# Merged gate and up products in the first SwiGLU, h stored by k-tile, half of the bias comparisons on ScalarE

## The chip, the cores and the metric

One NeuronCore of a Trainium2 chip runs the whole program in one launch. The metric is the device time of that launch in microseconds, the median of several runs. Engines are named as in the profile: PE (TensorE), DVE (VectorE), ACT (ScalarE), POOL (GpSimd), SP (SyncE, which issues most transfers).

## The reference

A decoder trunk of two layers on 256 tokens of width 1024, float32. Each layer is SwiGLU, token mixer, SwiGLU, every one behind an RMS norm and an adaLN shift, scale and gate computed from `c`:

```
h = modulate(rms_norm(x, g), shift, scale)
x = x + 0.5 * gate * ((silu(h @ w_gate) * (h @ w_up)) @ w_down)      # d_ff 2816, four of them
```

The mixer of layer 0 is causal attention with 16 heads and a T5 bias (32 buckets of the distance between positions, a learned row of 16 head values for each bucket); that of layer 1 is multi-head latent attention with a shared K/V. The adaLN vectors are `silu(c) @ ada_w`, eighteen products of a vector with a 1024x1024 matrix besides two for the shared K/V.

## The kernel before

All large products keep float32 accuracy by splitting both operands into a high part and a low part (`F32R`, the type that PE takes for the fast float32 pass): `hi` is an ACT copy rounded to the type (line 628 for weights, 772 for activations), `lo` is the DVE difference (lines 629, 773). A product is then hi·hi + hi·lo + lo·hi. Weights stream once from HBM through `raw` (3 buffers, 1 MB each), are split, and are used.

**SwiGLU (`ffn`, line 886).** The hidden dimension is done in tiles f of 128 rows, 22 of them. For a tile, gate and up are each a sum over 8 k-tiles of 128. The weight tile is stationary and h, transposed (features on partitions, 256 tokens in the free dimension), streams through. There are two ways to do one k-tile:

- `mm3` (line 756) makes three matmuls of 256 columns, all into one half of a PSUM bank (gate in one half, up in the other).
- `mm2` (line 860) makes a *merged* pair: w_hi against h_hi and h_lo side by side (512 columns, line 863), then w_lo against h_hi (256 columns, line 864) into the second half. A product then fills a whole bank, gate and up need two, and `units` (line 894) has to add the two halves: an ACT copy and a DVE addition for each (lines 904, 905).

`MERGED` (line 30) says which SwiGLUs are merged: three of four; the first one, (0, 0), is not. PSUM has four banks for these products (`ps_mm`, line 534).

`h` is one tile `[P, 2, NT, D]` (line 844): hi then lo, each with two halves of 128 tokens, each half 1024 wide by k. So the 512 columns of one k-tile lie in four runs of 128 elements, the 256 columns of one part in two.

**The first SwiGLU** starts in `first` (line 1481): tiles f0 to f5 while the first weights, the adaLN rows of (0, 0) and h are being made. Tiles f6 to f21 follow in the loop of line 944. In the same stretch the **bias** of the attention is built (`bias_steps`, line 1117): 64 DVE comparisons (line 1179, one for each of 32 keys in two blocks) write rows of zeros and ones in bfloat16, 288 small bfloat16 matmuls (line 1164, three for each comparison and query block) multiply them by a table of differences, ACT copies the result out (line 1168), POOL masks the diagonal, and it goes to DRAM.

**adaLN rows** are 512 KB transfers (line 655) and one DVE pass each (line 639 or 677), handed out evenly over PE's estimated time by `ada_pace` (line 712): 40 of them over 172 us in the first SwiGLU.

**Order.** `Order` (line 243) sorts every engine's instructions at build time with estimated durations, so the order on each engine is fixed when the program runs; an instruction whose input is late holds up all behind it on its engine.

Of the kernel before, what the change touches and what calls it, by code (L numbers as in the profile page):

```python
# [21 lines left out]
P = 128  # L22
# [7 lines left out]
MERGED = ((0, 1), (1, 0), (1, 1))  # L30
# [97 lines left out]
def lay_out(v):  # L128
# [37 lines left out]
    out["tab"] = np.concatenate([np.tile(table[1:], (4, 1)), np.tile(table[:-1], (4, 1)), *keys], axis=1)  # L166
# [356 lines left out]
def trunk(ctx: ExitStack, tc: tile.TileContext, a: dict, out: bass.AP):  # L523
# [304 lines left out]
    def split_h(h, c0, n, z):  # L828
        cs = slice(c0, c0 + n)
        h[2].update(range(c0 // P, (c0 + n) // P))  # L830
        return split_evac(h[0][:, cs], h[1][:, cs], z)
# [10 lines left out]
    def new_h(t):  # L842
        if t == 0:
            both = hp.tile([P, 2, NT, D], F32R, tag="h", name=nm("h"))
            pair[:] = [both[:, 0], both[:, 1], both]
        return pair[0][:, t, :], pair[1][:, t, :], set(), list(pair)

    def hk(h, k):
        until(lambda: k in h[2])
        return kslice(h[0], k), kslice(h[1], k)  # L850
# [35 lines left out]
    def ffn(layer, idx, h, after, ada_to, start=None):  # L886

        last = (layer, idx) == (1, 1)
        with ExitStack() as st:
# [4 lines left out]
            def units(f, gate, up=None):  # L894


                g = gp.tile([P, NT, P], F32, tag="gT", name=nm("g"), bufs=2)
                if up is None:
                    gate, up = gate[:, 0], gate[:, 1]
                    nc.scalar.activation(g, gate, AF.Silu)  # L900
                else:
                    u = gp.tile([P, NT, P], F32, tag="uT", name=nm("u"), bufs=2)
                    for x, ps in ((g, gate), (u, up)):
                        nc.scalar.activation(x, ps[:, 1], AF.Copy)
                        nc.vector.tensor_tensor(x, ps[:, 0], x, op=ALU.add)
# [3 lines left out]
                gh, gl = [gq.tile([P, NT, P], F32R, tag=f"{nme}{f}", name=nm(nme)) for nme in ("gh", "gl")]  # L909
                split_evac(gh, gl, g)  # L910
                for t in range(NT):
                    gT[f, t] = gh[:, t, :], gl[:, t, :]
# [3 lines left out]
            ada_pace(ada_to, 90.0 if last else FFN_PACE)  # L916
# [27 lines left out]
            for f0 in range(B1 * P if start else FB, F, S):  # L944
# [8 lines left out]
                for f in range(f0 // P, (f0 + S) // P):  # L953
                    merged = (layer, idx) in MERGED
                    ps = [mm_tile().rearrange("p (i t q) -> p i t q", i=2, q=P) for _ in range(1 + merged)]
                    for i, pl in enumerate(parts):
                        for k in range(KD):
# [6 lines left out]
                            else:  # L964
                                mm3(ps[0][:, i], *w, *hs[:2], start=k == 0, stop=k == KD - 1)
# [31 lines left out]
    def attention(ap, g, qTs, kTs, vs, bias, oT, state, after_s=None):  # L997
# [64 lines left out]
        def av():  # L1062
# [11 lines left out]
            pov = po.rearrange("p r t q -> p t r q")  # L1074
            hi, lo = [x[:, :, kk * P:(kk + 2) * P].rearrange("p t (r q) -> p t r q", q=P) for x in oT[0][3][:2]]
            split_evac(hi, lo, pov)
# [36 lines left out]
    pieces = [cp.tile([P, 4, H], BF16, name=f"tab{i}") for i in range(3)]  # L1113
# [3 lines left out]
    def bias_steps():  # L1117

# [4 lines left out]
        with ExitStack() as st:  # L1123
# [3 lines left out]
            btab = bp.tile([P, 2 * H + NT * NB], F32, name="btab")  # L1127
            nc.sync.dma_start(btab, a["tab"])
            tab, prev = btab[:, :H], btab[:, H:2 * H]
            keyi = btab[:, 2 * H:].bitcast(I32).rearrange("p (t b) -> p t b", t=NT)  # L1130
# [13 lines left out]
            V.tensor_scalar(key, keyi, least, None, op0=ALU.add)  # L1144
            yield

            def parts():
# [56 lines left out]
    def moba(h, after):  # L1204
        with ExitStack() as st:
# [15 lines left out]
            oTp = [ap.tile([P, NT, D], F32R, name=f"oT{i}") for i in range(2)]  # L1221
            oT = [(oTp[0][:, t, :], oTp[1][:, t, :], set(), oTp) for t in range(NT)]
# [258 lines left out]
    def first(units):  # L1481
# [5 lines left out]
        with ExitStack() as st:  # L1487
            fp = st.enter_context(tc.tile_pool(name="fp", bufs=1))
            zeros = fp.tile([P, 512], BF16, name="zeros")
# [40 lines left out]
            for f in range(B1):  # L1530
                nc.tensor.matmul(accs[f], zeros[:, :P], zeros, start=True, stop=False)
            accs = [ps.rearrange("p (i t q) -> p i t q", i=2, q=P) for ps in accs]
# [14 lines left out]
            def transposed(k):  # L1547
                xT = ps_x[k % 2][:, :S]
                with ranked(2 * k + 1):
# [8 lines left out]
                    for i in range(fill if k == 1 else 0):  # L1558
                        nc.tensor.matmul(kslice(xT, 1), zeros[:, :P], zeros[:, :P], start=False, stop=i == fill - 1)
# [3 lines left out]
            for k in range(KD):  # L1563
                with ranked(2 * k + 2):
# [5 lines left out]
                    hh, hl = [x[:, :, k * P:(k + 1) * P] for x in h0[0][3][:2]]  # L1570
                    split_evac(hh, hl, z.rearrange("p (t q) -> p t q", q=P))
# [68 lines left out]
```

## Time and profile before

| | us |
|---|---|
| runs before, median of 3 | 1007.17 (1007.09 to 1007.45) |
| the profiled execution | 1007.52 |
| its span | 1005.7 |
| PE busy | 992.3 (99%), granted clock full throughout |
| DVE busy | 846.3 (84%) |
| ACT busy | 610.9 (61%) |
| POOL busy | 85.6 (9%) |
| HBM read | 255.34 MB, 258 GB/s over the span |

A matmul's duration in the trace runs from its issue to the modelled end of its pipeline, so durations of neighbours overlap; what a matmul takes from PE's time is the distance from its start to the start of the next. For DVE the same holds to a smaller degree.

### The profile page before, as it was taken

Reading aid. Unit: us, or ns where it says so; the run is one execution under the profiler, and the core shown is the slowest. Engines: PE = TensorE matmul, PEld = TensorE weight load, DVE = VectorE, ACT = ScalarE, POOL = GpSimd, SP = SyncE. Lnnn points to the kernel's source line nnn. Section 1 sums busy time; section 2 is a strip of 40 time slices with the busy share of each in tenths; the row PEclk is TensorE's granted clock in tenths of the full one; section 3 lists DMA queues with packets and bytes.
Section 4 is the critical chain, followed back from the end, with each engine's and each line's share of the span. In section 5 each row is a group of like instructions: output and inputs, shape, how many; then the busy total and the mean of one; then the engine's idle time right before and its main releaser. Section 6 shows DMA issues by size and latency. Waiting matters only on the chain.

```text
span 1005.7 us, 15693 instructions
## 1 busy us (share of the span) xinstructions
PE 992.3 (99%) x5814; PEld 852.2 (85%) x5814; DVE 846.3 (84%) x1435; ACT 610.9 (61%) x1105; POOL 85.6 (9%) x124
## 2 busy tenths in 40 slices
PE   8999999999999999999999999999999999999998
PEld 6999998888888788888888888888888878888886
DVE  8999998799889899999889999854998789767642
ACT  5663754378756875665358566643879786566521
POOL 3011100022231000000000000000144010000000
PEclk9999999999999999999999999999999999999999
DMA  9978899889785679897988998553343467544630
GB/s 353 403 279 290 324 359 351 311 303 334 267 318 200 253 277 326 327 333 270 374 311 312 336 326 339 191 211 108 105 147 131 168 228 276 208 168 168 225 131 21
DMA packets 54238, 260.55 MB, mean 259 GB/s; under 512 B 6289, under 2 KB 6801, under 8 KB 35986
## 3 DMA queue, kind: packets, MB, share of 16 engines
q1 hardware_dynamic: 52850, 256.06, 70.0%
q0 software_dynamic: 1024, 3.17, 1.0%
q8 instruction: 45, 0.74, 0.3%
q10 hardware_dynamic: 288, 0.33, 0.1%
q14 instruction: 31, 0.25, 0.1%
HBM read 255.34 MB, written 4.19 MB: 258 GB/s over the span
## 4 chain that ended last, share of the span: by engine, by line
PE 90%; DVE 5%; DMA 4%; ACT 1%; issue 0%; SPq 0%; POOL 0%; ACTq 0%; DVEq 0%
PE mm L863 20%; PE mm L757 17%; PE mm L759 17%; PE mm L758 17%; PE mm L864 10%; PE at L1014 2%; DMA adaw<-in_ada_dram 1%; DMA raw<-in_first_dram 1%; PE at L1070 1%; PE at L1050 1%; PE tr L1164 1%; DVE lo L629 1%; DMA raw<-in_w_dram 1%; PE tr L807 1%; PE tr L1438 0%
## 5 line engine op out<-in xcount | busy, mean ns | idle before, releaser
L629 DVE TENSOR_TENSOR lo<-raw,hi 128x1024 fp32r<-128x1024 f32 (+3 forms) x312 | 368.3, 1200 | 80.0 <-ACT hi L628 79.5
L628 ACT ACTIVATE hi<-raw 128x1024 fp32r<-128x1024 f32 (+3 forms) x312 | 318.5, 1039 | 163.0 <-PE mm L759 123.3
L863 PE MATMUL mm<-h,hi 128*128 128x512 f32 x864 | 302.4, 398 | 0.0
L864 PE MATMUL mm<-h,lo 128*128 128x256 f32 x864 | 237.1, 281 | 0.0
L863 PEld LDWEIGHTS mm<-h,hi 128*128 128x128 f32 x864 | 160.7, 188 | 37.8
L864 PEld LDWEIGHTS mm<-h,lo 128*128 128x128 f32 x864 | 162.2, 189 | 2.4
L639 DVE CUSTOM_DVE_ANT_0 adaw<-adaw,c_b,cols 128x1024 f32<-128x1024 f32 x112 | 141.6, 1281 | 0.7 <-DMA adaw<-in_ada_dram 0.7
L757 PE MATMUL mm<-hi,gh 128*128 128x512 f32 x352 | 137.5, 391 | 0.0
L758 PE MATMUL mm<-lo,gh 128*128 128x512 f32 x352 | 137.1, 389 | 0.0
L759 PE MATMUL mm<-hi,gl 128*128 128x512 f32 x352 | 137.1, 389 | 0.0
L757 PE MATMUL mm<-hi,h 128*128 128x512 f32 (+1 forms) x240 | 94.6, 399 | 0.8 <-ACT h L772 0.8
L759 PE MATMUL mm<-hi,h 128*128 128x512 f32 (+1 forms) x240 | 92.7, 392 | 1.6 <-DVE h L773 1.6
L758 PE MATMUL mm<-lo,h 128*128 128x512 f32 (+1 forms) x240 | 93.6, 393 | 0.0
L759 PEld LDWEIGHTS mm<-hi,gl 128*128 128x128 f32 x352 | 66.1, 188 | 13.8
L757 PEld LDWEIGHTS mm<-hi,gh 128*128 128x128 f32 x352 | 66.1, 188 | 13.5
L758 PEld LDWEIGHTS mm<-lo,gh 128*128 128x128 f32 x352 | 66.1, 188 | 13.4
L757 PE MATMUL mm<-h,hi 128*128 128x256 f32 x256 | 73.3, 290 | 0.1
L759 PE MATMUL mm<-h,lo 128*128 128x256 f32 x256 | 72.8, 287 | 0.2 <-DVE lo L629 0.2
L758 PE MATMUL mm<-h,hi 128*128 128x256 f32 x256 | 72.3, 286 | 0.0
L677 DVE SCALAR_TENSOR_TENSOR acc<-adaw,cols,acc 128x1024 f32<-128x1024 f32 x48 | 62.3, 1298 | 0.1
L759 PEld LDWEIGHTS mm<-hi,h 128*128 128x128 f32 x240 | 45.1, 188 | 10.6 <-DVE h L773 2.2
L757 PEld LDWEIGHTS mm<-hi,h 128*128 128x128 f32 x240 | 45.1, 188 | 9.6 <-ACT h L772 1.3
(233 smaller groups left out, 1463.4 us busy)
## 6 DMA issues: line engine op xcount, KB each, us to landing
raw<-in_w_dram SPq DMA_DIRECT2D x142, 1024.0 KB, 5.7
adaw<-in_ada_dram SPq DMA_DIRECT2D x160, 512.0 KB, 6.0
raw<-in_first_dram SPq DMA_DIRECT2D x24, 256.0 KB, 7.6
raw<-in_w_dram SPq DMA_DIRECT2D x12, 512.0 KB, 3.5
raw<-in_w_dram SPq DMA_DIRECT2D x6, 576.0 KB, 3.9
bias_d<-bt SPq DMA_DIRECT2D x12, 256.0 KB, 4.4
bg<-bias_d POOLq DMA_DIRECT2D x4, 768.0 KB, 6.3
raw<-in_w_dram SPq DMA_DIRECT2D x2, 768.0 KB, 4.3
```

What stands on the lines that cost most here:

```text
L628: nc.scalar.activation(hi, src, AF.Copy)
L629: nc.vector.tensor_tensor(lo, src, hi.bitcast(F32), op=ALU.subtract)
L639: nc.vector.tensor_tensor_reduce(wt, wt, c_b, 1.0, cols[:, i, c:c + 1], op0=ALU.mult, op1=ALU.add, accum_out=m_cols[:, i, c:c + 1])
L677: nc.vector.scalar_tensor_tensor(acc, ada_tile(j, k), cact[:, k:k + 1], acc, op0=ALU.mult, op1=ALU.add)
L757: nc.tensor.matmul(ps, lh, rh, start=start, stop=False)
L758: nc.tensor.matmul(ps, lh, rl, start=False, stop=False)
L759: nc.tensor.matmul(ps, ll, rh, start=False, stop=stop)
L807: nc.tensor.transpose(kslice(pt, j), kslice(y, j), ident)
L863: nc.tensor.matmul(ps, wh, h[2], start=start, stop=False)
L864: nc.tensor.matmul(ps[:, 1], wl, h[0], start=False, stop=stop)
L1014: nc.tensor.matmul(ps3[:, i, :], qTs(e, t), kTs(e, nk), start=bias is not None, stop=bias is not None or i == len(es) - 1)
L1050: nc.tensor.transpose(kslice(pt, i * (t + 1) + kb), ss[u][:, i, kb * P:(kb + 1) * P], ident)
```

## The change

- `MERGED` takes in the first SwiGLU, so its tiles f6 to f21 are done by `mm2` with two banks each.
- `h` becomes one tile `[P, KD, 2, NT, P]`: for each k-tile, hi and lo with both halves of the tokens lie in one run of 512 elements. The attention output `oT` of layer 0 gets the same layout. `units`, `first` and `hk_both` follow.
- Every second bias comparison (odd i) is an ACT `Sign` of query position minus key, giving -1 or 1; its table rows are halved and the constant that this leaves is taken out through another table column set, so there are two sets of `pieces`.
- `ada_pace` hands out no adaLN row in the first 40 us of PE time after `first`.
- `u` has one buffer in the first SwiGLU in place of two, `zeros` is 128 wide.

```diff
-MERGED = ((0, 1), (1, 0), (1, 1))
+MERGED = ((0, 0), (0, 1), (1, 0), (1, 1))
...
-    def ada_pace(vectors, us):
+    def ada_pace(vectors, us, wait=0.0):
         n = vectors * KD - ada_done[0]
-        pace[0] = us / n if n > 0 else None
-        pace[1] = clock[0] + (us / n if n > 0 else 0.0)
+        pace[0] = (us - wait) / n if n > 0 else None
+        pace[1] = clock[0] + wait + (pace[0] or 0.0)
...
-            both = hp.tile([P, 2, NT, D], F32R, tag="h", name=nm("h"))
-            pair[:] = [both[:, 0], both[:, 1], both]
-        return pair[0][:, t, :], pair[1][:, t, :], set(), list(pair)
+            pair[:] = [hp.tile([P, KD, 2, NT, P], F32R, tag="h", name=nm("h"))]
+        return pair[0][:, :, 0, t], pair[0][:, :, 1, t], set(), pair[0]
...
-        hh, hl, both = h[0][3]
-        ks = slice(k * P, (k + 1) * P)
-        return hh[:, :, ks], hl[:, :, ks], both[:, :, :, ks]
+        both = h[0][3][:, k].rearrange("p i t q -> p (i t q)")
+        return both[:, :S], both[:, S:], both
...
-        nc.tensor.matmul(ps[:, 1], wl, h[0], start=False, stop=stop)
+        nc.tensor.matmul(ps[:, S:], wl, h[0], start=False, stop=stop)
...
-                    u = gp.tile([P, NT, P], F32, tag="uT", name=nm("u"), bufs=2)
+                    u = gp.tile([P, S], F32, tag="uT", name=nm("u"), bufs=1 if start else 2)
...
-            ada_pace(ada_to, 90.0 if last else FFN_PACE)
+            ada_pace(ada_to, 90.0 if last else FFN_PACE, 40.0 if start else 0.0)
...
+            below = bp.tile([P, NT, NB], F32, name="below")
+            V.tensor_scalar(below, key, -1.0, 0.5, op0=ALU.mult, op1=ALU.add)
...
+                for signs in range(2):
+                    rows = bp.tile([P, 4, H], F32, tag="rows", name=nm("rows"))
+                    if signs:
+                        V.tensor_tensor(tab, tab, end, op=ALU.subtract)
+                    V.scalar_tensor_tensor(rows, blk[:, :, None].to_broadcast([P, 4, H]), 0.5 if signs else 1.0,
+                                           tab[:, None, :].to_broadcast([P, 4, H]), op0=ALU.mult, op1=ALU.mult)
+                    for i in range(3):
+                        V.tensor_copy(pieces[signs][i], rows)
+                        if i < 2:
+                            V.tensor_tensor(rows, rows, pieces[signs][i], op=ALU.subtract)
...
-                             oh[:, i, (t - kb) * P:(t - kb + 1) * P], pieces[pi], start=pi == 0, stop=pi == 2)
+                             oh[:, i, (t - kb) * P:(t - kb + 1) * P], pieces[i % 2][pi], start=pi == 0, stop=pi == 2)
...
-                        V.tensor_scalar(oh[:, i], posq[:, kb * P:], key[:, kb, 8 * c + i:8 * c + i + 1],
-                             None, op0=ALU.is_ge)
+                        m = 8 * c + i
+                        if i % 2:
+                            nc.scalar.activation(oh[:, i], posq[:, kb * P:], AF.Sign, bias=below[:, kb, m:m + 1])
+                        else:
+                            V.tensor_scalar(oh[:, i], posq[:, kb * P:], key[:, kb, m:m + 1], None, op0=ALU.is_ge)
```

The order on the engines moves with it. Two places matter below. On PE, at the end of tile f7 of the first SwiGLU, before (`mm_856` is f7, `mm_1002` f8, `oh` the comparisons; lines 757 to 759 are `mm3`, 1164 the bias):

```order
L757 MATMUL mm_856<-h_112,hi_727 128x256
L758 MATMUL mm_856<-h_112,hi_727 128x256
L759 MATMUL mm_856<-h_112,lo_728 128x256
L757 MATMUL mm_1002<-h_112,hi_797 128x256
L1164 LDWEIGHTS oh_844
L1164 MATMUL tr_925<-tab_107,oh_844 128x64
L1164 LDWEIGHTS oh_844
L1164 MATMUL tr_925<-tab_108,oh_844 128x64
L757 MATMUL mm_856<-h_112,hi_727 128x256
```

and with the change (line 1169 is the bias, `mm_986` the gate of f8):

```order
L1169 MATMUL tr_1000<-tab_823,oh_867 128x64
L1169 LDWEIGHTS oh_867
L1169 MATMUL tr_1000<-tab_824,oh_867 128x64
L1169 LDWEIGHTS oh_867
L1169 MATMUL tr_1000<-tab_825,oh_867 128x64
L863 MATMUL mm_986<-h_109,hi_787 128x512
L864 MATMUL mm_986<-h_109,lo_788 128x256
L1169 LDWEIGHTS oh_867
L1169 MATMUL tr_1000<-tab_826,oh_867 128x64
```

Here 56 bias matmuls stand in one run between f7 and the first matmul of f8. Over the whole program the 288 bias matmuls stood in 45 runs before and stand in 17 now.

On DVE, around the first comparisons, before (`mm_710` is the bank of f6, whose only reader on DVE, line 908, stands 8 rows below this piece):

```order
L908 TENSOR_TENSOR g_702<-tr_190,g_702 128x256
L1179 TENSOR_SCALAR oh_844<-posq,key 128x256 x3
L1179 TENSOR_SCALAR oh_885<-posq,key 128x256
L1179 TENSOR_SCALAR oh_844<-posq,key 128x256
L1179 TENSOR_SCALAR oh_885<-posq,key 128x256
L1179 TENSOR_SCALAR oh_844<-posq,key 128x256
L1179 TENSOR_SCALAR oh_885<-posq,key 128x256 x5
L1179 TENSOR_SCALAR oh_990<-posq,key 128x256
L629 TENSOR_TENSOR lo_1006<-raw_1003,hi_1005 128x1024
L1179 TENSOR_SCALAR oh_885<-posq,key 128x256
L1179 TENSOR_SCALAR oh_990<-posq,key 128x256 x5
```

and with the change (`mm_707` and `mm_708` are gate and up of f6, `lo_792` and `lo_991` the next weights; line 630 is the weight split):

```order
L1188 TENSOR_SCALAR oh_828<-posq,key 128x256
L1188 TENSOR_SCALAR oh_867<-posq,key 128x256
L1188 TENSOR_SCALAR oh_828<-posq,key 128x256
L1188 TENSOR_SCALAR oh_867<-posq,key 128x256 x2
L905 TENSOR_TENSOR g_833<-mm_707,g_833 128x256
L1188 TENSOR_SCALAR oh_867<-posq,key 128x256
L1188 TENSOR_SCALAR oh_969<-posq,key 128x256 x2
L630 TENSOR_TENSOR lo_792<-raw_785,hi_791 128x1024
L630 TENSOR_TENSOR lo_991<-raw_988,hi_990 128x1024
L1188 TENSOR_SCALAR oh_969<-posq,key 128x256
L905 TENSOR_TENSOR u_834<-mm_708,u_834 128x256
```

The addition that empties the gate bank of f6 stands behind 21 small instructions, one line-908 product and 7 comparisons that follow `lo_788`, the first half of f8's gate weights.

## Rows read from the trace of the kernel before

**Rows 1.** The page, part 1: busy us, share of the span, instructions.

```profile
PE 992.3 (99%) x5814; PEld 852.2 (85%) x5814; DVE 846.3 (84%) x1435; ACT 610.9 (61%) x1105; POOL 85.6 (9%) x124
```

**Rows 2.** Waits of PE, the longest: who waited for whom, total us, times, longest.

```profile
PE mm L759 <- DVE h L773: 1.6, 2, 1.5
```

**Rows 3.** Windows: stretch, length, busy us of each engine, clock, DMA share, GB/s.

```profile
64.00:100.00 36.00, 36.00 (x484) 34.24 (x483) 34.53 (x84) 14.49 (x25) 6.77 (x7) 1.00 0.72 251
100.00:158.00 58.00, 58.00 (x483) 57.78 (x483) 55.80 (x101) 36.15 (x56) 3.25 (x3) 1.00 0.90 335
360.00:460.00 100.00, 100.00 (x567) 86.62 (x565) 96.76 (x148) 61.79 (x108) 2.98 (x4) 1.00 0.89 319
560.00:640.00 80.00, 80.00 (x454) 69.37 (x453) 77.70 (x122) 48.21 (x87) 0.00 (x0) 1.00 0.82 297
850.00:930.00 80.00, 80.00 (x455) 69.47 (x454) 57.66 (x89) 50.36 (x88) 0.00 (x0) 1.00 0.53 185
```

**Rows 4.** Timeline of PE, first SwiGLU, unmerged: start us, modelled duration us, instruction.

```profile
51.51 0.28 PE L757 MATMUL mm<-h,hi 128*128 128x256 f32 x1
...
124.78 0.28 PE L757 MATMUL mm<-h,hi 128*128 128x256 f32 x1
...
130.90 0.28 PE L757 MATMUL mm<-h,hi 128*128 128x256 f32 x1
...
157.90 0.40 PE L757 MATMUL mm<-hi,gh 128*128 128x512 f32 x1
```

**Rows 5.** Timeline of PE, second SwiGLU, merged pairs.

```profile
380.23 0.40 PE L863 MATMUL mm<-h,hi 128*128 128x512 f32 x1
380.46 0.28 PE L864 MATMUL mm<-h,lo 128*128 128x256 f32 x1
380.57 0.40 PE L863 MATMUL mm<-h,hi 128*128 128x512 f32 x1
...
385.88 0.40 PE L863 MATMUL mm<-h,hi 128*128 128x512 f32 x1
```

**Rows 6.** Timeline of PE, down product, 512 columns in one run.

```profile
479.65 0.39 PE L758 MATMUL mm<-lo,gh 128*128 128x512 f32 x1
...
483.95 0.39 PE L759 MATMUL mm<-hi,gl 128*128 128x512 f32 x1
```

**Rows 7.** Timeline of PE around runs of the bias matmuls.

```profile
64.10 0.20 PE L1164 MATMUL tr<-tab,oh 128*128 128x64 bf16 x1
64.14 0.36 PE L758 MATMUL mm<-h,hi 128*128 128x256 f32 x1
64.34 0.28 PE L757 MATMUL mm<-h,hi 128*128 128x256 f32 x1
64.46 0.61 PE L1164 MATMUL tr<-tab,oh 128*128 128x64 bf16 x15
64.91 0.36 PE L759 MATMUL mm<-h,lo 128*128 128x256 f32 x1
```

**Rows 8.** Timeline of DVE at the first comparisons.

```profile
60.63 1.22 DVE L629 TENSOR_TENSOR lo<-raw,hi 128x1024 fp32r<-128x1024 f32 x1
61.77 0.17 DVE L1150 TENSOR_TENSOR btab<-btab 128x16 f32<-128x16 f32 x1
...
62.48 0.35 DVE L1179 TENSOR_SCALAR oh<-posq,key 128x256 bf16<-128x256 f32 x1
62.75 0.22 DVE L1157 TENSOR_TENSOR rows<-rows,tab 128x64 f32<-128x64 f32 x1
...
64.00 0.42 DVE L908 TENSOR_TENSOR g<-tr,g 128x256 f32<-128x256 f32 x1
```

**Rows 9.** Groups by form: line, engine, shapes, count, busy us, mean ns.

```profile
L905 DVE TENSOR_TENSOR g<-mm,g 128x256 f32<-128x256 f32 x54 | 22.8, 422 | 4.5 <-ACT g L904 3.7
L904 ACT ACTIVATE g<-mm 128x256 f32<-128x256 f32 x54 | 20.7, 384 | 32.9 <-issue 19.0 <-PE mm L864 13.3
L772 ACT ACTIVATE gh<-g 128x256 fp32r<-128x256 f32 x76 | 31.0, 410 | 22.0 <-DVE g L908 21.3 <-issue 0.6
```

More of the change, by code (lines that the diff above doesn't have):

```diff
@@ L165, in lay_out @@
     keys = pos.view(np.float32).reshape(NT, NB, 4).transpose(0, 2, 1)[:, :, None].repeat(NB, axis=2).reshape(NT, P, NB)
-    out["tab"] = np.concatenate([np.tile(table[1:], (4, 1)), np.tile(table[:-1], (4, 1)), *keys], axis=1)
+    end = np.concatenate([table[-1:], np.zeros((NB - 1, H), np.float32)])
+    out["tab"] = np.concatenate([*[np.tile(x, (4, 1)) for x in (table[1:], table[:-1], end)], *keys], axis=1)
     for n in ("x", "c", "positions", "kv_a_norm_g", "mla_q_a_norm_g"):
@@ L828, in split_h @@
     def split_h(h, c0, n, z):
-        cs = slice(c0, c0 + n)
-        h[2].update(range(c0 // P, (c0 + n) // P))
-        return split_evac(h[0][:, cs], h[1][:, cs], z)
+        ks = slice(c0 // P, (c0 + n) // P)
+        h[2].update(range(ks.start, ks.stop))
+        return split_evac(h[0][:, ks], h[1][:, ks], z.rearrange("p (k q) -> p k q", q=P))
     def modulate_T(t, keys, r, wait):
@@ L954, in ffn @@
                     merged = (layer, idx) in MERGED
-                    ps = [mm_tile().rearrange("p (i t q) -> p i t q", i=2, q=P) for _ in range(1 + merged)]
+                    ps = [mm_tile() for _ in range(1 + merged)]
                     for i, pl in enumerate(parts):
@@ L1111, in trunk @@
     bias_d = dp.tile([3, P // NB, P, H * NB], F32, name="bias_d")
-    pieces = [cp.tile([P, 4, H], BF16, name=f"tab{i}") for i in range(3)]
     groups = []
@@ L1126, in bias_steps @@
             nc.sync.dma_start(posi, bcast_row(pos_f, S))
-            btab = bp.tile([P, 2 * H + NT * NB], F32, name="btab")
+            btab = bp.tile([P, 3 * H + NT * NB], F32, name="btab")
             nc.sync.dma_start(btab, a["tab"])
-            tab, prev = btab[:, :H], btab[:, H:2 * H]
-            keyi = btab[:, 2 * H:].bitcast(I32).rearrange("p (t b) -> p t b", t=NT)
+            tab, prev, end = [btab[:, i * H:(i + 1) * H] for i in range(3)]
+            keyi = btab[:, 3 * H:].bitcast(I32).rearrange("p (t b) -> p t b", t=NT)
             yield
@@ L1144, in bias_steps @@
             V.tensor_scalar(key, keyi, least, None, op0=ALU.add)
+            below = bp.tile([P, NT, NB], F32, name="below")
+            V.tensor_scalar(below, key, -1.0, 0.5, op0=ALU.mult, op1=ALU.add)
             yield
+            pieces = [[bp.tile([P, 4, H], BF16, name=f"tab{i}{j}") for j in range(3)] for i in range(2)]
             def parts():
@@ L1220, in moba @@
             nc.gpsimd.memset(qz[:DH, 1], 0.0)
-            oTp = [ap.tile([P, NT, D], F32R, name=f"oT{i}") for i in range(2)]
-            oT = [(oTp[0][:, t, :], oTp[1][:, t, :], set(), oTp) for t in range(NT)]
+            oTp = ap.tile([P, KD, 2, NT, P], F32R, name="oT")
+            oT = [(oTp[:, :, 0, t], oTp[:, :, 1, t], set(), oTp) for t in range(NT)]
             state, parts, qn, v = {}, {}, {}, {}
@@ L1530, in first @@
             for f in range(B1):
-                nc.tensor.matmul(accs[f], zeros[:, :P], zeros, start=True, stop=False)
-            accs = [ps.rearrange("p (i t q) -> p i t q", i=2, q=P) for ps in accs]
+                nc.tensor.matmul(accs[f], zeros, zeros[:, None].to_broadcast([P, 4, P]), start=True, stop=False)
             diag, rs, y, fill = [], [], {}, 10
@@ L1558, in transposed @@
                     for i in range(fill if k == 1 else 0):
-                        nc.tensor.matmul(kslice(xT, 1), zeros[:, :P], zeros[:, :P], start=False, stop=i == fill - 1)
+                        nc.tensor.matmul(kslice(xT, 1), zeros, zeros, start=False, stop=i == fill - 1)
                 return xT
@@ L1569, in first @@
                     nc.scalar.activation(z, xT[k], AF.Identity, scale=col_slice(1, key, k, 1), bias=col_slice(0, key, k, 1))
-                    hh, hl = [x[:, :, k * P:(k + 1) * P] for x in h0[0][3][:2]]
-                    split_evac(hh, hl, z.rearrange("p (t q) -> p t q", q=P))
+                    hh, hl = [h0[0][3][:, k, i].rearrange("p t q -> p (t q)") for i in range(2)]
+                    split_evac(hh, hl, z)
                 if k + 2 < KD:
@@ L1611, in q_norm @@
     def q_norm(t):
-        hkv[t] = (*(adap.tile([P, D], F32R, tag="acc" if t and g else "adaw", name=nm("hkv"), bufs=1 if t and g else 3)
-                    for g in range(2)), set())
+        parts = [adap.tile([P, D], F32R, tag="acc" if t and g else "adaw", name=nm("hkv"), bufs=1 if t and g else 3)
+                 for g in range(2)]
+        hkv[t] = *[x.rearrange("p (k q) -> p k q", q=P) for x in parts], set()
         hnext[t] = norm_T(t, (1, 1), ("kv", hkv[t]))
```

31 lines of the change are left out of this document (11 added, 20 removed).

## Prediction

> **What bounds the kernel now.** I read the page's busy times first: PE is busy 99% of the span [rows 1]. That alone could hide stalls, since a matmul's modelled duration runs past the next one's start, so I looked at PE's own waits. The longest entry is 1.6 us in two places [rows 2]; nothing there would repay removal. The windows say the same by stage: in the first, second, third and fourth SwiGLU PE is busy for the whole of each stretch, at the full clock (1.00), while DVE is at 96%, 97%, 97% and 72% [rows 3]. So the bound is PE's issue: what counts is the distance from one matmul's start to the next, and how many there are. A change is worth what it takes off that distance, unless it makes PE wait.
>
> **The distances.** An unmerged matmul of 256 columns takes 6.12 us / 51 = 0.120 us (from 124.78 to 130.90) [rows 4]. A merged pair takes 5.65 / 16 = 0.353 us (from 380.23 to 385.88), of which about 0.236 is the 512-column half and 0.117 the other [rows 5]. A 512-column matmul of the down product takes 4.30 / 19 = 0.226 us (479.65 to 483.95) [rows 6]. The last two stream the same number of columns of the same type with the same weight load; the difference that I can find is that h lies in four runs of 128 and the down product's operand in one run.
>
> **1. The merge in the first SwiGLU.** It has 16 tiles x 2 products x 8 k-tiles = 256 triples of 0.360 us. They become 256 pairs. If a pair costs 0.226 + 0.120 = 0.346 us [rows 4, 6], this saves 256 x 0.014 = 3.6 us; at today's pair of 0.353 [rows 5] it saves 1.8 us.
>
> A rule of the Trainium skill speaks against even this: "TensorE: Matmul & The Clock Gate" (Back-to-back issue gap) gives columns / 2.4 plus 2.5 ns for a matmul by itself, so dropping one of three would save 2.5 ns and the whole merge 0.6 us by estimate. Here the fixed part is 2 x 0.120 - 0.226 = 0.014 us [rows 4, 6]; the trace does not agree, and I use the trace.
>
> **2. The layout.** The other three SwiGLUs have 864 pairs (3 x 18 x 16). From 0.353 to 0.346 us saves 864 x 0.007 = 6.0 us [rows 4 to 6]. Bounds: nothing, if the runs don't matter; and 864 x 0.010 + 256 x 0.003 = 9.4 us if the 256-column half also keeps its 0.117. I take 6.0, because the 512-column row is the nearest. The writes of h now go out in pieces of 128; in the first SwiGLU they did so already, and I price that at nothing, hidden under PE.
>
> **3. Fewer switches between the two kinds of matmul.** A bias matmul takes 0.45 / 15 = 0.03 us, and the first float32 matmul behind a run of them takes 0.20 us in place of 0.12 (64.14 to 64.34), so a run costs 0.08 us [rows 7]. The order has 45 runs before and 17 now: 28 x 0.08 = 2.2 us saved. The 288 bias matmuls themselves stay (8.6 us).
>
> **4. Two banks for each tile.** Four PSUM banks held four tiles of the first SwiGLU and now hold two, so PE can run only one tile ahead of the additions that empty the banks, and these stand among comparisons on DVE. PE starts f6 at 51.51 [rows 4]; 32 pairs of 0.346 us bring it to 62.6, waits as before and the first eight bias matmuls to about 63.4. It then needs the bank of f6's gate. On DVE, the split that the order now calls `lo_788` takes the place of one that ended at 61.77, less one 0.42 us product and most of a split that now come later: about 60.9. Behind it stand 21 small instructions, 7 comparisons and a product. Before, 12 small ones and 3 comparisons took 2.23 us (61.77 to 64.00), a comparison 0.27 of it, so a small one 0.12 [rows 8]. That is 21 x 0.12 + 7 x 0.27 + 0.42 = 4.8 us, and the addition itself 0.42 [rows 9]: the bank is free at 66.1. Of the 2.7 us, 56 bias matmuls fill 1.7. So PE loses about 1.0 us, and some 0.5 more until the second weight half of f8 is split. From f9 on, the same count puts each bank free before PE needs it. I take a loss of 1.5 us; the bounds are nothing and, if DVE is late at each of the four tiles f8 to f11 by that 1.5, 6 us.
>
> **5. What costs nothing.** Half of the 64 comparisons leave DVE (32 x 0.27 = 8.6 us) and 32 additions come (13.5 us at 0.42 [rows 9]). With the adaLN rows put off, DVE's load falls while the bias is made and rises after it. ACT gets 32 `Sign` instructions and 32 copies; no row shows `Sign`, the nearest are ACT passes over 256 columns at 0.38 and 0.41 us [rows 9], so together at most 26 us, where ACT is idle for 43 of the 94 us from 64 to 158 [rows 3]. If that cover failed, the bill would appear as in point 4. The adaLN rows: the order has 23 of their transfers ahead of the 12th weight transfer where it had 28, and by the end of the stage three fewer than before; the down product has the room, and nothing reads them earlier. The later stages' orders differ in small ways; I price that at 0 plus or minus 1 us.
>
> **The sum.** -3.6 - 6.0 - 2.2 + 1.5 = -10.3 us against the profiled execution's own 1007.5, so 997.2; the median shown lies 0.3 below that execution, so **996.9 us**.
>
> **The rivals.**
> *The layout does nothing.* The 256-column matmuls also read h in two runs and take 0.120, which leaves no obvious extra for a run's end [rows 4]. Then the pair stays at 0.353: -1.8 - 2.2 + 1.5 = -2.5, 1004.7 us. Against it: nothing else that I can find separates the two 512-column distances [rows 5, 6]. The Trainium skill's "SBUF — State Buffer" (Door 1: The DMA port swizzle) sides with this rival: reads pay for crossing 16-byte lines with too few hits, and 128 float32 in a run fill their lines, so runs of that length should be free; the two distances [rows 5, 6] do not agree with it so far.
> *DVE takes it back in the second and third SwiGLU.* It is at 97% there [rows 3]; a PE that is 2% faster needs it at 99%. If it can't, two thirds of point 2 (4.0 us) go: 1000.9 us. For: the narrow margin. Against: the adaLN rows are not due until the stage's end and the down product leaves DVE room.
> *Slower: banks in the whole first SwiGLU.* If every one of its 16 tiles waits w for its additions, 16 w stands against 11.8 us of gains, and beyond w = 0.86 us the kernel is slower by over 2 us. At w = 1.0 it is 1007.2 + 16.0 - 11.8 = 1011.4 us. For: DVE is at 96% there, and additions are queued behind comparisons and weight splits. Against: the other three work with two banks a tile at no wait [rows 3], and comparisons end by f11.
> *The change doesn't do what it says:* the order shows 256 more pairs and 768 fewer matmuls of 256 columns, so no.
>
> **Chances.** Forecast (996.9 give or take 2.5) 0.60; the pair even shorter, down to 992.5, 0.06; DVE takes it back 0.08; layout does nothing 0.19; slower 0.07. The range 992.5 to 1005.0 leaves out the slower rival and the worse part of the layout's. A measurement here tells some 0.2% (2 us) from no change, so the border is 1005.2: the layout rival at 1004.7 falls half on each side. Faster 0.83, same 0.10, slower 0.07.
>
> **What would show it.** The pairs of the second SwiGLU at 0.346 us start to start (0.353: point 2 is wrong). About 1120 pairs and no 256-column triples outside `first`; 88.6 us for the first SwiGLU's pairs where 92.2 stood. Bias matmuls in runs of 24, one switch for each. A gap of 1 to 2 us on PE near 65 us that ends on the addition of line 905. DVE near 99% in the second and third SwiGLU without waits of PE on the weight split. The forecast is wrong if PE shows new waits of over 5 us in all, or if the three later gate and up stretches are not 2% shorter.

## The result, and the profile after

The changed kernel takes 1001.71 us (median of 6 runs, 999.42 to 1002.69) against 1007.17 (1007.09 to 1007.45): ratio 0.9944, interval [0.9931, 0.9957], so about 5.5 us faster. The forecast was 996.9 us; its sign held, its size did not. The profiled execution took 1002.69 us, its span is 1000.9 us, 4.8 below the span before.

The page, parts 1 and 4 (busy us, share and instructions of each engine; the chain of waits by engine) and the two merged lines of part 5, after:

```profile
PE 986.4 (99%) x5558; PEld 836.7 (84%) x5558; DVE 850.1 (85%) x1443; ACT 629.1 (63%) x1169; POOL 82.5 (8%) x124
...
PE 78%; issue 9%; DVE 7%; DMA 4%; ACT 1%; POOL 0%; SPq 0%; DVEq 0%; ACTq 0%; POOLq 0%
...
L863 PE MATMUL mm<-h,hi 128*128 128x512 f32 x1120 | 391.8, 397 | 1.1 <-DVE u L905 0.6
L864 PE MATMUL mm<-h,lo 128*128 128x256 f32 x1120 | 306.5, 280 | 0.0
```

Against [rows 1] PE has 256 matmuls fewer, DVE 3.8 us more and ACT 18.2 us more. There are the 1120 pairs that the prediction counted. The chain's 9% of `issue` is mostly one piece of 85.65 us from 124.17 us on, for which the chain names no releaser; PE is busy for all of these 85.65 us, so it is not idle time of PE. What bounds the kernel is read from the windows instead: the stretches of [rows 3], with one more ahead of them (columns as there):

```profile
48.00:64.00 16.00, 15.55 (x102) 13.33 (x100) 15.62 (x47) 12.96 (x26) 1.12 (x32) 1.00 0.98 374
64.00:100.00 36.00, 35.91 (x433) 30.96 (x432) 35.95 (x75) 32.50 (x73) 7.75 (x8) 1.00 0.78 269
100.00:158.00 58.00, 57.40 (x323) 49.69 (x322) 56.91 (x103) 36.43 (x65) 1.50 (x2) 1.00 0.91 323
360.00:460.00 100.00, 100.00 (x577) 87.40 (x576) 98.50 (x151) 63.48 (x111) 3.00 (x4) 1.00 0.88 317
560.00:640.00 80.00, 80.00 (x455) 69.44 (x454) 77.69 (x119) 48.69 (x86) 0.00 (x0) 1.00 0.85 304
850.00:930.00 80.00, 80.00 (x456) 69.56 (x455) 56.65 (x87) 49.97 (x87) 0.00 (x0) 1.00 0.53 187
```

The first of these windows in the kernel before:

```profile
48.00:64.00 16.00, 15.69 (x130) 15.24 (x128) 15.65 (x40) 11.03 (x19) 1.12 (x32) 1.00 0.98 380
```

PE is still busy for nearly all of each stretch, so its issue is still the bound, and two things stand in the rows. In the first SwiGLU PE now idles 0.45 + 0.09 + 0.60 = 1.1 us, where it idled 0.3 us before. And in the last two rows PE has as many instructions as in [rows 3] (455 against 454, 456 against 455): nothing got denser in the third and fourth SwiGLU. In 360:460 there are 10 more.

The same by stage, from PE's timeline: from the first gate or up matmul of a SwiGLU (behind `first`) to its first down matmul, and the mean distance of its merged pairs, each taken from one 512-column start to the next where records are complete.

| stretch | before, us | after, us | difference | forecast | pair before, ns | pair after, ns |
|---|---|---|---|---|---|---|
| first SwiGLU | 106.4 | 102.9 | -3.4 | -4.3 | (three of 120) | 349.6 |
| second | 103.9 | 102.3 | -1.6 | -2.0 | 352.9 | 346.6 |
| third | 102.8 | 102.8 | 0 | -2.0 | 352.5 | 352.3 |
| fourth | 102.5 | 102.5 | 0 | -2.0 | 351.2 | 351.2 |
| all else | | | +0.2 | 0 | | |

Of the 5.5 us that are missing from the forecast in this execution (10.3 less 4.8), 4 lie in the third and fourth SwiGLU, where the layout changed and the pair did not. Those means hide what the timeline shows: there are two paces. After, in the second SwiGLU (PE's timeline: start us, modelled duration us, instruction), 16 pairs in 5.55 us, 0.347 each:

```profile
380.21 0.40 PE L863 MATMUL mm<-h,hi 128*128 128x512 f32 x1
380.44 0.28 PE L864 MATMUL mm<-h,lo 128*128 128x256 f32 x1
380.56 0.39 PE L863 MATMUL mm<-h,hi 128*128 128x512 f32 x1
...
385.76 0.40 PE L863 MATMUL mm<-h,hi 128*128 128x512 f32 x1
```

After, in the third, 11 pairs in 3.89 us, 0.354 each, with the new layout:

```profile
599.82 0.40 PE L863 MATMUL mm<-h,hi 128*128 128x512 f32 x1
...
603.71 0.40 PE L863 MATMUL mm<-h,hi 128*128 128x512 f32 x1
```

And before the change, late in the fourth, 13 pairs in 4.50 us, 0.346 each, with h in four runs of 128:

```profile
913.90 0.39 PE L863 MATMUL mm<-h,hi 128*128 128x512 f32 x1
914.13 0.27 PE L864 MATMUL mm<-h,lo 128*128 128x256 f32 x1
914.24 0.40 PE L863 MATMUL mm<-h,hi 128*128 128x512 f32 x1
...
918.40 0.40 PE L863 MATMUL mm<-h,hi 128*128 128x512 f32 x1
```

So each layout is seen at each pace, the last one in a trace that lay open before the change was timed; [rows 5] come from one of its slow stretches.

### The profile page after: what moved, and what is told of

Its sections match the earlier page's. It is cut to its first block, busy times and chain, and to the rows that moved or that the text cites. A ratio compares the mean times of both kernels' runs of the same rounds, so it can differ in the third digit from the quotient of the medians.

```text
span 1000.9 us, 15247 instructions
## 1 busy us (share of the span) xinstructions
PE 986.4 (99%) x5558; PEld 836.7 (84%) x5558; DVE 850.1 (85%) x1443; ACT 629.1 (63%) x1169; POOL 82.5 (8%) x124
## 4 chain that ended last, share of the span: by engine, by line
PE 78%; issue 9%; DVE 7%; DMA 4%; ACT 1%; POOL 0%; SPq 0%; DVEq 0%; ACTq 0%; POOLq 0%
PE mm L863 23%; PE mm L759 12%; PE mm L761 12%; PE mm L760 12%; PE mm L864 11%; DVE lo L630 2%; PE at L1014 2%; DMA adaw<-in_ada_dram 2%; DMA raw<-in_first_dram 1%; PE at L1070 1%; PE at L1050 1%; PE tr L809 1%; DMA raw<-in_w_dram 1%; PE tr L1169 1%; DVE z L825 0%
## 5 line engine op out<-in xcount | busy, mean ns | idle before, releaser
L863 PE MATMUL mm<-h,hi 128*128 128x512 f32 x1120 | 391.8, 397 | 1.1 <-DVE u L905 0.6
L864 PE MATMUL mm<-h,lo 128*128 128x256 f32 x1120 | 306.5, 280 | 0.0
L863 PEld LDWEIGHTS mm<-h,hi 128*128 128x128 f32 x1120 | 208.1, 188 | 48.5 <-DVE u L905 1.1
L864 PEld LDWEIGHTS mm<-h,lo 128*128 128x128 f32 x1120 | 210.1, 188 | 3.5 <-DVE lo L630 0.3
L761 PEld LDWEIGHTS mm<-hi,gl 128*128 128x128 f32 x352 | 66.1, 188 | 13.7
L759 PEld LDWEIGHTS mm<-hi,gh 128*128 128x128 f32 x352 | 66.1, 188 | 13.6
L760 PEld LDWEIGHTS mm<-lo,gh 128*128 128x128 f32 x352 | 66.1, 188 | 13.5
L760 PEld LDWEIGHTS mm<-lo,h 128*128 128x128 f32 x240 | 45.1, 188 | 8.0 <-issue 0.2
L904 ACT ACTIVATE g<-mm 128x256 f32<-128x256 f32 x70 | 26.7, 382 | 35.1 <-issue 18.1
L904 ACT ACTIVATE u<-mm 128x256 f32<-128x256 f32 x70 | 26.6, 380 | 35.2 <-PE mm L864 33.9
```

The lines of the kernel that those rows point to most:

```text
L759: nc.tensor.matmul(ps, lh, rh, start=start, stop=False)
L760: nc.tensor.matmul(ps, lh, rl, start=False, stop=False)
L761: nc.tensor.matmul(ps, ll, rh, start=False, stop=stop)
L864: nc.tensor.matmul(ps[:, S:], wl, h[0], start=False, stop=stop)
L904: nc.scalar.activation(x, ps[:, S:], AF.Copy)
```

## The experiments

Twelve kernels, in three sessions with the kernel before beside them (medians 1007.54, 1007.69 and 1007.69). The theory at the start was that the pace belongs to the layout; the rival, that the layout does nothing and the gain is the first SwiGLU's.

**The change without its other parts, and the other parts without it.** `layout_only` takes the new layout alone; `all_but_layout` is the change with h back in `[P, 2, NT, D]`.

```diff
-MERGED = ((0, 0), (0, 1), (1, 0), (1, 1))
+MERGED = ((0, 1), (1, 0), (1, 1))
...
-            ada_pace(ada_to, 90.0 if last else FFN_PACE, 40.0 if start else 0.0)
+            ada_pace(ada_to, 90.0 if last else FFN_PACE, 0.0)
...
-                        if i % 2:
-                            nc.scalar.activation(oh[:, i], posq[:, kb * P:], AF.Sign, bias=below[:, kb, m:m + 1])
-                        else:
-                            V.tensor_scalar(oh[:, i], posq[:, kb * P:], key[:, kb, m:m + 1], None, op0=ALU.is_ge)
+                        V.tensor_scalar(oh[:, i], posq[:, kb * P:], key[:, kb, m:m + 1], None, op0=ALU.is_ge)
```

> The kernel before with the new layout of h and of the attention output alone (first SwiGLU unmerged, comparisons on VectorE, adaLN rows as before). Theory A, my forecast's: the layout sets the pair's distance, so all 864 pairs take 0.3467 us in place of 0.3533 and the time is 1007.2 - 5.8 = 1001.4 us. Theory B: the pair has two paces, 0.3467 and 0.3533, whatever the layout, and each long stretch of pairs keeps the one in which it was entered; then single stretches of the second, third and fourth SwiGLU stand at either pace, and the time lies between 1001.4 and 1007.2 us, each stretch of some 230 pairs being worth 1.5 us. Under B the layout itself is worth nothing; under A no pair is at 0.3533.

Measured 1005.33 us (1004.84 to 1006.91, 11 runs), ratio 0.9983 [0.9974, 0.9992]: 1.7 us faster by the ratio, 2.2 by the medians. The runs stand in two groups, six from 1004.84 to 1005.33 and five from 1006.45 to 1006.91.

```diff
-            pair[:] = [hp.tile([P, KD, 2, NT, P], F32R, tag="h", name=nm("h"))]
+            both = hp.tile([P, 2, NT, D], F32R, tag="h", name=nm("h"))
+            pair[:] = [both.rearrange("p i t (k q) -> p k i t q", q=P)]
```

> The changed kernel with the old layout of h (four runs of 128 for the 512 columns) and everything else as changed. Theory A: all 1120 pairs at 0.3533 us, so about 0.0066 x 1120 = 7.4 us above a kernel with every pair at 0.3467; against the changed kernel, where some 330 pairs ran at 0.3467 in the profile, 2 us more: 1003.9 us. Theory B: stretches at 0.3467 are found with the old layout as well, and the time is within 2 us of the changed kernel's 1001.7.

Measured 1003.40 us (1002.05 to 1004.25), ratio 0.9960 [0.9946, 0.9973], an interval that overlaps that of the whole change. PE's timeline of `all_but_layout`, four runs of 128, second SwiGLU: 16 pairs in 5.55 us, as with the new layout.

```profile
380.19 0.39 PE L865 MATMUL mm<-h,hi 128*128 128x512 f32 x1
...
385.74 0.39 PE L865 MATMUL mm<-h,hi 128*128 128x512 f32 x1
```

Its four mean pairs are 349.6, 346.7, 352.2 and 351.3 ns, those of the change to 0.1 ns. And of `layout_only`, one run of 512, late in the fourth: 11 pairs in 3.88 us, 0.353 each, where the kernel before has 0.346.

```profile
913.90 0.40 PE L863 MATMUL mm<-h,hi 128*128 128x512 f32 x1
...
917.78 0.40 PE L863 MATMUL mm<-h,hi 128*128 128x512 f32 x1
```

The layout does not set the pace: the first theory falls. In its profile `layout_only` gains 1.6 us in the second SwiGLU, which runs at the fast pace (346.9 ns), and loses 0.5 us again at the end of the fourth. Its span is 2.6 us shorter than that of the kernel before; some 1.3 us of this lie outside the four stretches, and no run says why. So the edit does move the time a little, with an interval clear of no change, though not by what a pair costs in either layout.

**The merge alone, and with one aid each.** `merge_only` is the old layout with the merge, the comparisons all on DVE and the adaLN rows not put off (`u` has one buffer there, as in the change); `all_but_sign` and `all_but_pace` are the whole change less one of the two aids (the first takes the last piece of the diff of `layout_only`, the second its middle piece).

> The kernel before with the first SwiGLU merged and nothing else (old layout, all 64 comparisons on VectorE, adaLN rows handed out from the start). The order has 32 runs of bias matmuls where it had 45 (13 x 0.08 = 1.0 us saved). Theory A: pairs at 0.3533, 1.8 us saved, and a loss on the banks of 1.5 us or more, since VectorE has the additions on top of all comparisons and adaLN rows: 1005 to 1008 us. Theory B: between 1.8 and 3.5 us saved by the merge, as the pace falls. If the put-off rows and ScalarE's comparisons are what makes the merge possible, TensorE waits for additions of line 905 by more than 3 us in the first SwiGLU here.

Measured 1012.49 us (1011.06 to 1013.62), ratio 1.0050 [1.0037, 1.0062]: 5 us slower than before, outside both ranges expected. Its first SwiGLU takes 111.2 us. The waits for additions (line 907 in this kernel) come to 0.9 us in all there and not to over 3. PE's longest wait is another, shown here with PE's timeline around it:

```profile
PE mm L866 <- DVE lo L630: 2.5, 2, 2.3
```

```profile
100.79 0.40 PE L865 MATMUL mm<-h,hi 128*128 128x512 f32 x1
103.44 0.38 PE L866 MATMUL mm<-h,lo 128*128 128x256 f32 x1 [2.26 <-DVE lo L630]
...
104.62 0.63 PE L865 MATMUL mm<-h,hi 128*128 128x512 f32 x1
105.05 0.41 PE L866 MATMUL mm<-h,lo 128*128 128x256 f32 x1
```

DVE's timeline at the same time says who was in front of that weight split:

```profile
99.14 1.27 DVE L678 SCALAR_TENSOR_TENSOR acc<-adaw,cols,acc 128x1024 f32<-128x1024 f32 x1
100.33 0.72 DVE L1312 SCALAR_TENSOR_TENSOR ang<-kk,ang 128x32 f32<-128x32 f32 x1
100.98 1.27 DVE L678 SCALAR_TENSOR_TENSOR acc<-adaw,cols,acc 128x1024 f32<-128x1024 f32 x1
102.17 1.21 DVE L630 TENSOR_TENSOR lo<-raw,hi 128x1024 fp32r<-128x1024 f32 x1
```

Two adaLN passes and a small instruction, 3 us, stand ahead of it. And the windows show a second bill behind the wait: the granted clock (third column from the end) falls to 0.50, the lower of its two levels (1.2 GHz in place of 2.4), and the 512-column matmul at 104.62 takes 0.43 us to its neighbour, where it takes 0.23 at the full clock.

```profile
102.00:104.00 2.00, 0.56 (x3) 0.51 (x4) 2.00 (x5) 1.72 (x2) 0.00 (x0) 1.00 0.84 310
104.00:106.00 2.00, 2.00 (x11) 1.34 (x9) 2.00 (x2) 1.81 (x4) 0.89 (x1) 0.61 1.11 365
106.00:108.00 2.00, 1.31 (x3) 0.83 (x3) 2.00 (x5) 1.65 (x3) 0.60 (x2) 0.50 0.93 389
108.00:110.00 2.00, 2.00 (x9) 1.55 (x8) 1.98 (x4) 2.00 (x5) 0.00 (x0) 0.50 0.63 178
110.00:112.00 2.00, 2.00 (x9) 1.70 (x8) 2.00 (x5) 1.71 (x4) 0.00 (x0) 0.68 0.94 389
112.00:114.00 2.00, 2.00 (x13) 1.75 (x12) 2.00 (x5) 1.31 (x3) 0.00 (x0) 1.00 0.57 135
```

Over 100 to 125 us the granted clock is 0.86 in the mean, which by estimate costs 25 x 0.14 = 3.5 us. PE idles 4.4 us in this stage against 1.1 in the change, and 15 more runs of bias matmuls cost 15 x 0.08 = 1.2 us by the price of [rows 7]. By these estimates 3.5 + 3.3 + 1.2 = 8.0 of the 8.2 us are accounted for between the two kernels' first SwiGLUs.

> The changed kernel with all 64 comparisons back on VectorE. If ScalarE's half matters only through the number of runs of bias matmuls (30 here, 17 with it, 45 before), this kernel is 13 x 0.08 = 1.0 us slower than the changed one: 1002.7 us. If it matters because VectorE is the bound from 64 to 100 us, the first SwiGLU is longer by up to the 8.6 us of comparisons that return there: up to 1010 us, with waits of TensorE for line 905 and for the weight split.

Measured 1004.13 us (1002.76 to 1005.23), ratio 0.9965 [0.9953, 0.9978]; its first SwiGLU takes 103.8 us. That is near the first of the two cases, 1.4 us above it.

> The changed kernel with the adaLN rows of the first SwiGLU handed out from the start, as before (no 40 us of delay); ScalarE still makes half of the comparisons. With both aids the first SwiGLU took 102.9 us, without the comparisons on ScalarE 103.8 us, without either 111.2 us. If the two aids do the same thing (room on VectorE before 100 us), either alone is nearly enough, and this kernel is within 2 us of the changed one: 1001.7 to 1003.7 us. If the delay is what matters, the first SwiGLU is near 111 us here too, and the time 1008 to 1010 us.

Measured 1004.72 us (1003.31 to 1005.54), ratio 0.9972 [0.9960, 0.9984]; its first SwiGLU takes 103.3 us. The time is 1.0 us above the range of the first case and far from the second. Either aid alone thus takes away most of the 8.2 us between `merge_only` (111.2) and the change (102.9); the second one adds 0.4 to 0.9 us in these profiles. By the whole time the interval of `all_but_sign` overlaps those of the two others, while those of the change (up to 0.9957) and of `all_but_pace` (from 0.9960) just miss each other; the profile of `all_but_pace` is its fastest run, and what its slower runs lose, no trace shows. The bias matmuls stand in 30 runs in `all_but_sign` and in 17 in `all_but_pace`, so the bundling comes with ACT's half of the comparisons.

**What else could set the pace.** The merged pair's second matmul writes the upper half of its bank; `first_half` writes the lower one (the halves are added afterwards anyway).

```diff
-        nc.tensor.matmul(ps[:, S:], wl, h[0], start=False, stop=stop)
+        nc.tensor.matmul(ps[:, :S], wl, h[0], start=False, stop=stop)
```

> The changed kernel with the 256-column matmul adding to the first half of the bank in place of the second (the same sum, since the halves are added later). If the long pace came from where in the PSUM bank the short matmul writes, all stretches stand at one pace here, 0.3467 or 0.3533. Under theories B and C nothing changes: stretches at either pace, and the time between 999 and 1003 us.

One run, 1002.79 us. Its mean pairs are 349.6, 346.7, 352.3 and 346.9 ns: three as after the change, the fourth SwiGLU at the fast pace but for a piece from 902.6 to 908 us. Both paces are still there, so the half of the bank is not what makes them.

The other way to test it is the order of the two matmuls. `swap_odd` puts the 256-column one first in every odd k-tile, so that equal ones stand in twos; `two_by_two` issues two of 512 and then two of 256.

```diff
+        if odd:
+            nc.tensor.matmul(ps[:, S:], wl, h[0], start=False, stop=False)
-        nc.tensor.matmul(ps, wh, h[2], start=start, stop=False)
-        nc.tensor.matmul(ps[:, S:], wl, h[0], start=False, stop=stop)
+        nc.tensor.matmul(ps, wh, h[2], start=start, stop=stop and odd)
+        if not odd:
+            nc.tensor.matmul(ps[:, S:], wl, h[0], start=False, stop=stop)
```

> The changed kernel with every second pair turned round: 512, 256, 256, 512, 512, 256, 256, 512 columns. Theory C: as with two by two, no stretch at the long pace: two pairs in 0.693 us in all four SwiGLUs. Theory D: 0.700 us for two pairs in slow stretches. If the pace is nothing to do with the order inside the pair, some stretches stay at 0.707 us for two.

One run, 1000.35 us; three periods of two pairs take 2.09 us at 380.67 and 2.09 at 600.66, 0.348 a pair. Over complete periods the means of its four SwiGLUs are 348.4 to 349.2 ns.

```diff
-        nc.tensor.matmul(ps[:, S:], wl, h[0], start=False, stop=stop)
+        kept.append((wl, h[0]))
+        if len(kept) == 2:
+            for n, (w, hh) in enumerate(kept):
+                nc.tensor.matmul(ps[:, S:], w, hh, start=False, stop=stop and n == 1)
+            kept.clear()
```

> The changed kernel with the four matmuls of two neighbouring k-tiles in the order 512, 512, 256, 256 columns in place of 512, 256, 512, 256. Theory C: the long pace (0.3533) is a state that strict alternation carries on; without it no stretch is at it, two pairs take 0.693 us everywhere, and the profile's some 460 pairs at the long pace give 3 us: 998.6 us, with less spread from run to run. Theory D: the extra is paid at each 256-column matmul that hands over to a 512-column one, in whatever order; half as many hand-overs then pay half: 0.700 us for two pairs in the slow stretches, and 1.5 us in all: 1000.2 us.

Measured 1000.51 us (1000.17 to 1002.60), ratio 0.9934 [0.9921, 0.9946]. PE's timeline of `two_by_two` in the second and in the third SwiGLU: 10 pairs in 3.48 us, and 8 in 2.79.

```profile
380.51 0.63 PE L865 MATMUL mm<-h,hi 128*128 128x512 f32 x2
380.97 0.40 PE L869 MATMUL mm<-h,lo 128*128 128x256 f32 x2
...
383.99 0.63 PE L865 MATMUL mm<-h,hi 128*128 128x512 f32 x2
...
600.44 0.63 PE L865 MATMUL mm<-h,hi 128*128 128x512 f32 x2
...
603.23 0.63 PE L865 MATMUL mm<-h,hi 128*128 128x512 f32 x2
```

Both are 0.348, and over complete periods the means of the four SwiGLUs are 348.3 to 348.9 ns: with equal matmuls in twos the stages no longer differ. Neither theory is met as it stood: C had 0.3465 everywhere and D 0.350 in slow stretches only; the time lies near D's 1000.2. Its four gate and up stretches take 101.9, 102.7, 101.7 and 101.7 us. The pace is thus a matter of the order in which the two lengths follow each other, and the slow pace can be kept away by it. Its interval overlaps that of the change (0.9931 to 0.9957), so that it beats the change is likely from its stretches and not shown by the medians.

**Longer groups.** `four_by_four` and `eight_by_eight` carry the same edit with 4 and 8; `eight_old_layout` is `eight_by_eight` with the old layout; `before_eight` is the kernel before with groups of 8 and nothing else.

> The same with groups of four: 0.3467 + 0.0033 / 4 = 0.3475 us for a pair if the extra belongs to the cycle of 512s and 256s, so 0.9 us less than two by two: 999.6 us. If eight by eight is slower than this one, it is because the low parts or the banks are held longer.

Measured 1004.30 us (1003.63 to 1005.33), ratio 0.9967 [0.9955, 0.9979]: missed by 4.7 us. Groups of four pairs take 1.40 us (350.0 to 351.2 ns a pair in the four SwiGLUs, over complete groups), and the start of the first stretch is 1.3 us late (53.05 us against 51.71).

> The changed kernel with the eight 512-column matmuls of a product first and its eight 256-column ones behind them, so one hand-over in eight pairs. Two by two and the swapped pairs ran at one pace everywhere, 0.3483 us for a pair, 0.0033 us for each cycle of 512s and 256s over the sum of the two widths (0.3467). If the extra belongs to the cycle, a pair takes 0.3467 + 0.0033 / 8 = 0.3471 us in all four SwiGLUs, 1.4 us less than two by two: 999.1 us. If it belongs to the pair, the time is two by two's 1000.5 us.

Measured 1002.17 us (1001.48 to 1003.41), ratio 0.9945 [0.9933, 0.9957]: missed by 3 us. A group of eight pairs takes 2.79 us, 0.349 a pair (PE's timeline of `eight_by_eight`, third SwiGLU; the window ends with the first matmul of the next eight):

```profile
600.17 1.12 PE L869 MATMUL mm<-h,lo 128*128 128x256 f32 x8
601.12 2.00 PE L865 MATMUL mm<-h,hi 128*128 128x512 f32 x8
602.96 0.28 PE L869 MATMUL mm<-h,lo 128*128 128x256 f32 x1
```

The expectation took the fast pace, 0.3467, for the sum of the two lengths; in the groups the 512-column matmul takes 0.230 and the other 0.119, 0.349 in all. Besides, there are new waits in the first SwiGLU, where the additions of line 905 (911 in this kernel) now come late (PE's waits):

```profile
PE mm L865 <- DVE u L911: 1.4, 1, 1.4
...
PE mm L865 <- DVE g L911: 1.0, 1, 1.0
```

> Eight by eight with the old layout of h (512 columns in four runs of 128). With no alternation left, the layout stands alone: if four runs cost anything, a pair is longer than eight by eight's in all stretches (0.3533 would be my forecast's price, 7 us in all); if they cost nothing, the pair takes the same 0.347 us and the two kernels agree within 1 us.

Measured 1003.75 us (1000.57 to 1005.65, 6 runs), ratio 0.9958 [0.9944, 0.9972]. The medians lie 1.6 us apart, not within 1, but the runs spread over 5 us; the profiles decide better: over complete groups 349.2 to 349.7 ns a pair in the four SwiGLUs with either layout, and the second to fourth gate and up stretches take 102.95, 101.96 and 101.96 us in both. With the pace held by the order, the layout is again worth nothing.

> The kernel before with eight by eight in its three merged SwiGLUs and nothing else. Its profile had some 760 of 864 pairs at 0.3533 us. If the long pace is what alternation carries on and the layout is nothing, these go to 0.3471 and 760 x 0.0062 = 4.7 us are saved: 1002.7 us. If the layout is needed as well, it stays within 1 us of the kernel before.

Measured 1004.77 us (1004.49 to 1005.16), ratio 0.9971 [0.9960, 0.9981]: 2.9 us faster than before, by the order of the matmuls alone, where 4.7 were expected. Its three merged stretches run at 349.2, 349.5 and 349.6 ns where the kernel before has 352.9, 352.5 and 351.2. Over 288 pairs each, 288 x (3.7 + 3.0 + 1.6) ns = 2.4 us, which is most of it. What is missing from the 4.7 is mostly that a pair takes 349 ns and not the 347.1 expected.

## Why the prediction was right or wrong

**1. The merge.** The mechanism is right, the size smaller. A pair costs 349.6 ns on average in the first SwiGLU, not 346, so 256 x 10.4 ns = 2.7 us in place of 3.6. The 0.346 that was added up from [rows 4, 6] is what a pair takes in a fast stretch; a part of this stretch (131 to 155 us) ran at 353. That the sum meets the fast pace is partly chance, since in groups of eight the two lengths are 0.230 and 0.119 and not 0.226 and 0.120. The Trainium skill's "TensorE: Matmul & The Clock Gate" (Back-to-back issue gap) has a fixed part of 2.5 ns for an isolated matmul; the trace does not agree for this merge, which saves 10.4 ns a triple.

**2. The layout. This is the step that failed.** The prediction held that "nothing else that I can find separates the two 512-column distances". Something else does: the pair has two paces, 0.347 and 0.353, that belong to stretches and not to layouts. The one window read for [rows 5] was slow; the same trace at 914 us would have shown the old layout at 0.346. The forecast of 6.0 us became 1.6, and even these came with no help of the layout (`all_but_layout` has the same 346.7 ns in the second SwiGLU). The rival "the layout does nothing" was right about the layout, but it too knew only one pace and left the pair at 0.353 everywhere. The measured 1001.71 us lies between the two, inside the range of 992.5 to 1005.0, and that is luck: neither had the second pace, which gave the 1.6 us. The Trainium skill's "SBUF — State Buffer" (Door 1: The DMA port swizzle), by which runs of 128 float32 fill their lines and should be free, had sided with it; now the trace agrees, with 349.2 to 349.7 ns a pair in either layout.

**3. The switches.** The count is as forecast, and so is the price. PE's timeline after, at the end of f7:

```profile
64.21 0.23 PE L1169 MATMUL tr<-tab,oh 128*128 128x64 bf16 x2
64.28 0.36 PE L864 MATMUL mm<-h,lo 128*128 128x256 f32 x1
64.48 1.95 PE L1169 MATMUL tr<-tab,oh 128*128 128x64 bf16 x56
66.31 0.50 PE L863 MATMUL mm<-h,hi 128*128 128x512 f32 x1
66.64 0.28 PE L864 MATMUL mm<-h,lo 128*128 128x256 f32 x1
```

The 256-column matmul behind a short run takes 0.20 us in place of 0.12, the 512-column one behind the long run 0.33 in place of 0.235: 0.08 and 0.09 a run, and 56 small ones pass in 1.83 us, as at 0.03 each. No run isolates the 2.2 us.

**4. Two banks.** The bank was free when the prediction said. DVE's timeline after:

```profile
65.83 0.42 DVE L905 TENSOR_TENSOR g<-mm,g 128x256 f32<-128x256 f32 x1
```

That ends at 66.25, against 66.1 forecast. But PE had started this stretch 0.2 us later, waited 0.45 us just before 55.15 (for a weight's high part, `hi` of line 629) and paid four short runs of bias matmuls on its way, so the 56 in one run began at 64.48 and not at about 63.4, and filled the whole wait. The idle time moved elsewhere: the waits of PE after the change have

```profile
PE mm L863 <- DVE u L905: 0.6, 1, 0.6
PE mm L863 <- ACT hi L629: 0.5, 1, 0.5
```

with the first of them at 122 us, where the prediction had counted no bank late. In all that is 1.1 us of idle time by the windows; 0.3 us stood in the same windows before, so 0.8 are new, against 1.5 forecast. That the size came out near is luck, since the place did not hold. With 2.7 + 2.2 - 0.8 = 4.1 against 3.4 measured, the first SwiGLU is accounted for to 0.7 us, with the 2.2 us for the switches taken as priced.

**5. What costs nothing.** It cost nothing: `Sign` took 12.6 us of ACT in all (the groups by form after, line 1186, 256 and 128 wide),

```profile
L1186 ACT ACTIVATE oh<-posq,below 128x256 bf16<-128x256 f32 x16 | 6.9, 507 | 0.0
...
L1186 ACT ACTIVATE oh<-posq,below 128x128 bf16<-128x128 f32 x16 | 5.7, 404 | 0.0
```

and ACT rose by 18.2 us where at most 26 were allowed. But the point is incomplete: these two parts are what the merge lives on. Without both of them it loses 5 us instead of gaining.

**The rivals.** "DVE takes it back" fell: in 360:460 DVE is busy 98.50 of 100 us, PE all 100, and the pairs ran at 0.347. The third stayed slow after the change, but in `all_but_sign` its pairs ran at 0.347 too, with DVE busy 78.91 of the 80 us from 560 on and PE all 80. "Slower: banks in the whole first SwiGLU" did not come, but `merge_only` shows how near it was: 1012.5 us, close to the rival's 1011.4, by a weight split that stood behind adaLN passes and not by the additions.

**Open.** What decides which pace a stretch takes is not settled. In the straight part of the second SwiGLU the kernel before and the changed one issue the same matmuls in the same order, one at 0.353 and one at 0.347, both at the full granted clock; in the places looked at, the pace changed where something else stands among the pairs (near a stretch's end, where the adaLN sums of lines 688 and 689 are and some lengths follow themselves). The larger spread of most changed kernels (999.42 to 1002.69 us after; the kernel before spreads over 0.4 us beside it and 1.0 to 1.2 us in the later sessions) would fit stretches that change pace from run to run, some 230 pairs x 6.7 ns = 1.5 us each, and so would the two groups of `layout_only`, some 1.5 us apart. But no trace of a run of its slower group was kept, and `two_by_two` spreads over 2.4 us and `eight_old_layout` over 5 with a uniform pace in their profiles, so that is argued at best.

## What to carry to other kernels

Read the distance from start to start in several stretches of the same loop before putting a price on it: one window here gave a pair that was 2% too slow, and a layout was credited with the difference. When long and short matmuls alternate, try them in twos; that is a small edit and gave one pace in all four SwiGLUs here (0.348 to 0.349), while longer groups gave a slightly slower one and later evacuations. And when a PE-bound stage is made denser, look first at what stands ahead of the weight splits on DVE: with the same merge the first SwiGLU grew by 4.8 us with that queue as it was, and shrank by 2.6 to 3.4 once rows, comparisons or both were taken out of it.

## What the runs showed of the hardware

- The alternating pair of 512 and 256 columns has two steady paces, 0.347 and 0.353 us, at the full granted clock. Grouped in twos it takes 0.348 to 0.349 (means of the four SwiGLUs), in fours 0.350 to 0.351, in eights 0.349 to 0.350, with no second pace.
- One wait of 2.26 us on PE in `merge_only` was followed by a granted clock of 0.50 from 106 to 110 us (0.61 and 0.68 in the windows beside it), which over 100 to 125 us makes a mean of 0.86: by estimate a loss of 25 x 0.14 = 3.5 us, more than the wait itself. PE had been busy 0.56 us of the 2 us before it fell. After the change, with a longest merged wait of 0.6 us, the clock stays at 1.00 in every window shown.
